# A two-layer convolution trunk on one core: stores of prepared weights and results moved to ScalarE's queue, layer 1's outputs moved behind its products

## The chip, the cores and the metric

One core of a Trainium2 chip runs the whole program in one launch. The metric is device time in microseconds (us), the median of three runs. The profile is one further execution of the same program.

## What is computed

x is 2048 rows by 1024 columns, c one row of 1024; all is float32. Two layers, then the output:

```python
cond = silu(c)
for l in (0, 1):
    shift, scale, gate = split(cond @ ada_w[l] + ada_b[l])      # 1024 each
    u = x * (1 + scale) + shift
    if l == 0:                                                  # "A"
        a, g, z = split(u @ W_in + b_in)                        # three of 1024 columns
        h = conv31(a * sigmoid(g)) + b_conv                     # causal, depthwise
        y = (silu(layer_norm(h)) * silu(z)) @ W_out + b_out
    else:                                                       # "B"
        b, c_, v, z = split(u @ W_in)                           # four of 1024 columns
        y = (b * conv3(c_ * v) * silu(z)) @ W_out
    x = layer_norm(sqrt(2) * x + gate * y) * g_post + b_post
```

## The kernel before

**Layout.** Columns lie on the 128 partitions, rows along the free axis. The 2048 rows are cut into two halves sc = 0, 1, each half into its even and its odd rows, which makes four quarters q = 2 sc + hf of T = 512 rows. The 1024 columns are 8 blocks of 128.

**A product.** Each matrix is done with one level of Strassen's scheme: a pair of column blocks (`Pair`, lines 236 to 348) needs 7 products instead of 8, of sums and differences of weight blocks (`make`, lines 255 to 293) and of sums and differences of u (`u_first`, `u_second`, lines 213 to 231: b11, b21, t1, t2, b22, t3, t4). Each operand is split into two float32r parts, hi by ScalarE and lo = operand - hi (`split`, line 184), so one product (`product`, line 350) is 4 blocks by 3 matmuls, 12 matmuls of 128x128 by 128x512. Layer A has 12 pairs of 7 products per half (8 pairs "a", 4 pairs "z"), layer B has 16 (8 "c", 8 "b"). The products write banks x, y, z of PSUM, of which there are four under the tag mm. After a product, `evacuate` (line 313) copies a bank with ScalarE or adds it with VectorE.

**Weights.** A pair's seven weight operands are built once, in half 0, from two raw loads (tag raw, 4 buffers), into buffers of the tag w (5 buffers), and stored to `kept` (line 291); half 1 loads them back. The sums of weight blocks run on GpSimd for layer A and on VectorE for layer B (`self.adds`, lines 245 and 982).

**The convolution of 31 taps** is cut into even and odd rows (`conv_a`, lines 457 to 543): 41 multiply-adds of VectorE for each of 8 blocks and each half (`mac`, line 467), with a few steps on ScalarE and GpSimd. They stand in a list, `todo`; `tick` (line 92) emits some of them after each product: 3 for layers A and B, 1 for an output step (`RATE`, line 34). When a block's accumulators are done, `statistics` (line 548) transposes them on TensorE and takes their sums on VectorE. When all 8 blocks of a quarter are done, `a_norm` (line 618) normalises it.

**Outputs.** `mixer_out` (lines 678 to 765) multiplies a quarter by W_out, 2 halves by 8 blocks by 12 matmuls, so 16 groups of the size of a product, adds the residual rows, normalises and stores; in layer 0 it also transposes the result (`columns`) into layer 1's u. W_out is first multiplied by the gate and split (`fold_gate`, line 425) into `w_dram`. `ada_sum` (line 397) makes a row of the modulation; both run as a background generator, one step for each product.

**Order of the program.** Start (lines 854 to 873): four rounds i, each with the loads of ada_w (`adak`), `modulation_a(i)` (line 373, 32 matmuls of one column), transposes of x, `u_parts`, and the first three products of pair 0 for the block before. Then the products of A for half 0 (A0), the input of half 1 (`u_half`, four times between the last products), A for half 1 (A1), outputs of quarters 0 and 1 of layer 0, B for half 0 (B0, with the gate of layer 1 folded in the background), then output of quarter 0 of layer 1, quarters 2 and 3 of layer 0, quarter 1 of layer 1, B for half 1 (B1), quarters 2 and 3 of layer 1.

**Queues.** Every transfer, loads and stores, is issued by SyncE (`load`, line 64, and `store`, line 73). Each engine and each queue works through its instructions in order. The order on all engines but TensorE is set by a scheduler from the order in the text, with `urgent` parts (line 76) first; TensorE keeps the order of the text.

## Time and profile before

| | us |
|---|---|
| median of 3 runs (1825.81 to 1827.89) | 1826.01 |
| the profiled execution | 1821.89 |
| its span, first to last instruction | 1820.1 |
| TensorE busy | 1602.8 (88%) |
| VectorE busy | 1161.4 (64%) |
| GpSimd busy | 1001.6 (55%) |
| ScalarE busy | 662.3 (36%) |

TensorE's mean granted clock is 0.941. The 16 transfer engines are busy 74.5% with the one queue that the kernel uses. A busy TensorE is no measure of how fast it works, since its matmuls take twice as long at the lower clock; so the stretches are read against the number of products in them.

### The profile page before, as it was taken

How to read it: one execution, taken by the hardware profiler on the slowest of the kernel's cores; microseconds unless marked ns; L12 is line 12 of the kernel's file. 1: busy time of each engine (PE TensorE's matmuls, PEld its weight loads, DVE VectorE, ACT ScalarE, POOL GpSimd, SP SyncE). 2: the span in 40 equal slices, each digit the busy share in tenths (PEclk: the TensorE clock that was granted, in tenths of full speed). 3: DMA queues.
4: the chain of work that ended last, by engine and by line, in shares of the span. 5: the costliest groups of instructions: out<-in, count | busy, mean ns of one | idle time of the engine just before them, and what ended most of it. 6: DMA issues, size and time to landing. Idle time of an engine off the chain costs nothing.

```text
span 1820.1 us, 21371 instructions
## 1 busy us (share of the span) xinstructions
PE 1602.8 (88%) x6956; PEld 1303.9 (72%) x6956; DVE 1161.4 (64%) x1737; ACT 662.3 (36%) x1134; POOL 1001.6 (55%) x868
## 2 busy tenths in 40 slices
PE   4989998789797977849878789998898999999995
PEld 4968787668676866737656568876677788888784
DVE  2329999978685899488988776457556321221264
ACT  2335455563342243464433233423643111111221
POOL 4268889476653254768877777727864211111243
PEclk9789999889898998979999899999999999999998
DMA  6558888779896896736777788899876666666865
GB/s 185 178 193 301 298 296 323 252 261 359 323 394 196 288 336 229 234 145 206 263 252 273 248 300 290 285 350 337 311 262 205 205 207 208 203 209 209 314 246 194
DMA packets 230719, 471.76 MB, mean 259 GB/s; under 512 B 20312, under 2 KB 94416, under 8 KB 230608
## 3 DMA queue, kind: packets, MB, share of 16 engines
q1 hardware_dynamic: 230608, 470.40, 74.5%
q8 instruction: 55, 0.90, 0.2%
q14 instruction: 56, 0.46, 0.1%
HBM read 299.81 MB, written 170.52 MB: 258 GB/s over the span
## 4 chain that ended last, share of the span: by engine, by line
PE 49%; DVE 18%; DMA 13%; POOL 10%; issue 6%; ACT 3%; SPq 1%; POOLq 0%; DVEq 0%; ACTq 0%
PE po L80 9%; PE pxc L80 7%; PE pxb L80 6%; PE pxa L80 6%; DVE pca L467 4%; PE pzc L80 4%; PE pzb L80 3%; PE pza L80 3%; DVE pcb L467 3%; PE pxz L80 2%; PE pm L80 2%; PE pya L80 2%; PE pyb L80 1%; PE pyc L80 1%; DMA wr<-w_dram 1%
## 5 line engine op out<-in xcount | busy, mean ns | idle before, releaser
L467 DVE SCALAR_TENSOR_TENSOR pcb<-h,w,pcb 128x512 f32<-128x512 f32 x224 | 166.7, 744 | 6.6 <-ACT pcb L475 6.4
L467 DVE SCALAR_TENSOR_TENSOR pca<-h,w,pca 128x512 f32<-128x512 f32 x192 | 142.9, 744 | 0.2
L467 DVE SCALAR_TENSOR_TENSOR pca<-xs,w,pca 128x512 f32<-128x512 f32 x128 | 95.6, 746 | 0.3
L728 DVE TENSOR_TENSOR r<-po,r 128x512 f32<-128x512 f32 x64 | 43.2, 679 | 80.0 <-issue 33.0
L793 POOL TENSOR_TENSOR hb1c<-c12c,c22c 128x512 f32<-128x512 f32 x16 | 22.1, 1384 | 130.9 <-DVE c22c L326 130.9
L467 DVE SCALAR_TENSOR_TENSOR pcd<-xs,w,pcd 128x512 f32<-128x512 f32 x112 | 83.5, 745 | 3.1 <-ACT pcd L509 3.1
L706 ACT ACTIVATE r<-r,nb,rs 128x512 f32<-128x512 f32 x64 | 47.7, 807 | 90.0 <-DVE nb L701 90.0
L412 POOL TENSOR_TENSOR ada<-ada,adaw 128x512 f32<-128x512 f32 x48 | 64.9, 1354 | 12.0 <-ACT adaw L406 10.2
L80 PE MATMUL pm<-cond,adak 128*128 128x1 f32 x256 | 49.0, 327 | 19.6 <-DMA adak<-in_ada_w_dram 19.6
L80 PEld LDWEIGHTS pm<-cond,adak 128*128 128x128 f32 x256 | 48.9, 298 | 20.3 <-DVE ua00t L220 10.1
L186 POOL TENSOR_TENSOR wa<-rawa,wa 128x512 fp32r<-128x512 f32 x32 | 42.1, 1322 | 28.0 <-ACT wa L185 28.0
L442 POOL TENSOR_TENSOR wf<-wf,grow 128x512 f32<-128x512 f32 x32 | 43.8, 1374 | 23.1 <-DMA wf<-in_b_w_out_dram 11.7
L481 POOL TENSOR_TENSOR lead<-lead,part 128x512 f32<-128x512 f32 x32 | 42.8, 1337 | 20.7 <-ACT part L480 20.7
L406 ACT ACTIVATE adaw<-adaw,cond 128x512 f32<-128x512 f32 x64 | 42.7, 715 | 31.6 <-DMA adaw<-in_ada_w_dram 25.9
L694 POOL TENSOR_TENSOR r<-r,gb 128x512 f32<-128x512 f32 x32 | 42.1, 1330 | 21.4 <-DVE pcb L467 11.0
L707 POOL TENSOR_TENSOR r<-r,g 128x512 f32<-128x512 f32 x32 | 49.8, 1566 | 3.9 <-ACT r L706 3.9
L721 ACT ACTIVATE ub<-ptx,sh,sc 128x128 f32<-128x128 f32 x128 | 46.7, 472 | 14.0 <-PE ptx L83 14.0
L186 POOL TENSOR_TENSOR wc<-rawc,wc 128x512 fp32r<-128x512 f32 x32 | 43.5, 1360 | 13.0 <-ACT wc L185 12.6
L186 POOL TENSOR_TENSOR wb<-rawb,wb 128x512 fp32r<-128x512 f32 x32 | 43.1, 1347 | 11.9 <-ACT wb L185 11.9
L647 ACT ACTIVATE v<-v,second_columns 128x512 f32<-128x512 f32 x32 | 25.8, 814 | 61.8 <-DVE v L646 51.5
L708 POOL TENSOR_TENSOR r<-r,b 128x512 f32<-128x512 f32 x32 | 47.7, 1499 | 0.6
L186 POOL TENSOR_TENSOR wf<-wf 128x512 fp32r<-128x512 f32 x32 | 43.9, 1377 | 6.2 <-ACT wf L185 6.2
(1385 smaller groups left out, 5570.5 us busy)
## 6 DMA issues: line engine op xcount, KB each, us to landing
wr<-w_dram SPq DMA_DIRECT2D x128, 512.0 KB, 5.1
kepta<-wa SPq DMA_DIRECT2D x56, 512.0 KB, 4.8
wa<-kepta SPq DMA_DIRECT2D x56, 512.0 KB, 6.5
keptc<-wc SPq DMA_DIRECT2D x56, 512.0 KB, 3.2
keptb<-wb SPq DMA_DIRECT2D x56, 512.0 KB, 4.5
wc<-keptc SPq DMA_DIRECT2D x56, 512.0 KB, 4.4
wb<-keptb SPq DMA_DIRECT2D x56, 512.0 KB, 4.3
adaw<-in_ada_w_dram SPq DMA_DIRECT2D x32, 512.0 KB, 7.2
```

Source lines behind the costliest of these rows:

```text
L80: return tc.keep_in_program_order(nc.tensor.matmul(*args, **kw))
L186: (eng or nc.gpsimd).tensor_tensor(lo, src, hi.bitcast(F32), op=ALU.subtract)
L406: nc.scalar.activation(raw[:, j], raw[:, j], AF.Identity, scale=cond[:, kk + j:kk + j + 1])
L412: nc.gpsimd.tensor_tensor(acc, acc, raw[:, j], op=ALU.add)
L442: nc.gpsimd.tensor_tensor(w[:, 1], w[:, 1], grow, op=ALU.mult)
L467: nc.vector.scalar_tensor_tensor(out=tiles[out], in0=src, scalar=w, in1=tiles[acc], op0=ALU.mult, op1=op)
L481: nc.gpsimd.tensor_tensor(lead, lead, part, op=ALU.add)
L706: nc.scalar.activation(r, r, AF.Identity, scale=rs, bias=nb)
L707: eng.tensor_tensor(r, r, g[h], op=ALU.mult)
L708: eng.tensor_tensor(r, r, b[h], op=ALU.add)
L721: nc.scalar.activation(fs[k][:, t * P:(t + 1) * P], pt[:, j * P:(j + 1) * P], AF.Identity, scale=sc1[:, k:k + 1], bias=sh1[:, k:k + 1])
L728: nc.vector.tensor_tensor(r, pss[t], r, op=ALU.add)
```

## The change

Seven things are changed together.

1. `store_late` and `flush`: the stores of kept weights, of `h_dram`, `z_dram`, `cc_dram`, `gb_dram` and `w_dram` (326 in all) are collected and issued by ScalarE, behind the next evacuation or activation in the text. The stores of accumulators and of output rows stay with SyncE. The zero windows of `h_dram` (16 stores) move in the text to the end of the start.
2. `modulation_a`: VectorE multiplies four of the eight blocks by cond and adds them; TensorE does the other four and the sum, 20 matmuls in place of 32. Each adak load holds one block of rows and both m.
3. The input of x is loaded in blocks of one column block (`u_block`). For half 1 its 16 blocks are spread over the last eleven products of A0 (`second_u`, `moves`); the last two pairs of every list are interleaved (`order_of`); four products, not three, run beside the start (`early`). The rows of the tables of columns and taps are loaded a round or more ahead, into the tag acc, not uf.
4. The subtraction for t2 moves from VectorE to GpSimd (`u_second`). In layer 1, `u_stages` makes all t1, then all t2, and so on, on VectorE and GpSimd in turn, and six products of B stand ahead of it in place of four.
5. In B0, two of the four weight sums of a pair move from VectorE to GpSimd. The second raw load of a pair is issued when its first sum is due.
6. The rate of the convolution is 3.2 steps a product in A, 3.4 in B; h has one buffer in place of two. `a_norm` of a half's first quarter runs within the last eleven products (`ending`), and the transposes of an output in layer 0 come 9 and 6 ticks behind its rows, not 6 and 4. The background of A1 takes two ticks for each step of `ada_sum`.
7. Layer 1's gate is folded during B1, and all four quarters of layer 1 are put out after B1.

```diff
+    def store_late(dst, src, then=None):
+        late.append((dst, src, then))
+    def flush(after=None):
+        with ExitStack() as order:
+            if after is not None:
+                order.enter_context(tc.issue_after(after.ins))
+            for dst, src, _ in late:
+                nc.scalar.dma_start(dst, src)
+        for *_, then in late:
+            if then is not None:
+                then()
+        late.clear()
...
-BUFS = dict(u=56, raw=4, s=1, w=5, ta=8, hin=2, xs=1, pt=1, acc=3, tv=2, uf=6)
+BUFS = dict(u=56, raw=4, s=1, w=5, ta=8, hin=1, xk=2, xs=1, pt=1, acc=3, tv=2, uf=6)
-RATE = dict(a=3, b=3, o=1)
+RATE = dict(a=3.2, b=3.4, o=1)
...
-                store(keep[n], wt.bitcast(F32))
+                store_late(keep[n], wt.bitcast(F32))
...
-                    nc.scalar.copy(t[key], bk[b])
+                    done = nc.scalar.copy(t[key], bk[b])
...
+                flush(done)
...
     def modulation_a(i):
         pm = bank("conv", f"pm{i}")
+        raws = []
+        for j in range(K):
+            raw = st("u", [P, 2, 2 * P], f"adak{i}_{j}")
+            load(raw, ada_w[0, j * P:(j + 1) * P, :2 * D].rearrange("p (m d) -> p m d", m=2)
+                 [:, :, 2 * i * P:(2 * i + 2) * P])
+            raws.append(raw)
+        acc = raws[0]
+        with urgent():
+            nc.vector.tensor_scalar(acc, acc, cond[:, :1], None, op0=ALU.mult)
+            for j in range(1, 4):
+                nc.vector.scalar_tensor_tensor(out=acc, in0=raws[j], scalar=cond[:, j:j + 1],
+                                               in1=acc, op0=ALU.mult, op1=ALU.add)
         for m in range(2):
             for b in range(2):
                 o = m * 2 + b
-                for j in range(K):
...
+                for j in range(4, K):
+                    matmul(pm[:, o:o + 1], raws[j][:, m, b * P:(b + 1) * P],
+                           cond[:, j:j + 1], start=(j == 4), stop=False)
+                matmul(pm[:, o:o + 1], acc[:, m, b * P:(b + 1) * P], ones[:, :1],
+                       start=False, stop=True)
...
-            U["t2"].append(u_tile(b11, name + "t2", nc.vector))
+            U["t2"].append(u_tile(b11, name + "t2"))
...
-                    tt(s, a12, s, op=ALU.subtract)
+                    tt2(s, a12, s, op=ALU.subtract)
...
-                    tt(a11, a11, a21, op=ALU.subtract)
+                    tt2(a11, a11, a21, op=ALU.subtract)
...
+        c, a, b = n - 3, n - 2, n - 1
+        return seq + [(c, 3), (a, 1), (c, 7), (b, 1), (c, 4)] + [
+            (a, 2), (b, 2), (a, 5), (a, 6), (a, 3), (b, 5), (b, 6), (b, 3),
+            (a, 7), (b, 7), (a, 4), (b, 4)]
...
+    moves = {(late_b, 2): 2, (late_a, 5): 2, (late_a, 6): 1, (late_a, 3): 1, (late_b, 5): 1,
+             (late_b, 6): 1, (late_b, 3): 2, (late_a, 7): 1, (late_b, 7): 1, (late_a, 4): 2,
+             (late_b, 4): 2}
...
+    for pair in pb[0]:
+        pair.adds = (nc.vector, nc.gpsimd)
+    rows = ending(pb[0], with_join(0, order_b), RATE["b"], 2)
+    need(3)
+    run_out(0, 2, wait(6, norms[3]))
+    begin_out(3, 0, rows)
+    run_out(0, 3, wait(10, join_first(1)))
     back = background_b()
+    for n, (p, r) in enumerate(with_join(1, order_b)):
+        if (p, r) == (n_b - 1, 5):
+            rows = out_rows(0, 1)
...
+        product(pb[1][p], r)
+        tick(0, *([back] if n > 8 else ()))
+    flush()
+    for q in range(NQ):
         begin_out(q, 1, rows)
+        if q:
+            b_gate(q, gs[1, q])
         run_out(1, q)
```

**SyncE's queue at the start**, round 0 to round 1 (adak is ada_w, xkua is x, rawa raw weights, kepta the store of a prepared weight). Before:

```order
L71 DMA rawa0_0_1_253<-in_a_w_in_dram 128x8x128
L74 DMA kepta0_0_250<-wa0_0_1_256 128x1024
L74 DMA kepta0_0_250<-wa0_0_2_260 128x1024
L74 DMA kepta0_0_250<-wa0_0_5_265 128x1024
L74 DMA kepta0_0_250<-wa0_0_6_687 128x1024
L71 DMA adak1_0_0_270<-in_ada_w_dram 128x2x256
```

Now:

```order
L71 DMA rawa0_0_1_239<-in_a_w_in_dram 128x8x128
L74 DMA h_dram0_89<-zero_104 128x15 x2
L74 DMA h_dram1_90<-zero_104 128x15 x2
L74 DMA h_dram2_91<-zero_104 128x15 x2
L74 DMA h_dram3_92<-zero_104 128x15 x2
L74 DMA h_dram4_93<-zero_104 128x15 x2
L74 DMA h_dram5_94<-zero_104 128x15 x2
L74 DMA h_dram6_95<-zero_104 128x15 x2
L74 DMA h_dram7_96<-zero_104 128x15 x2
L71 DMA adak1_0_247<-in_ada_w_dram 128x2x256
```

The four weight stores no longer stand ahead of round 1's ada_w; the 16 zero stores, which stood ahead of round 0's, stand there now.

**VectorE at the start**, round 0 to round 1 (ua00 is u of round 0, mod0 the modulation). Before:

```order
L220 TENSOR_TENSOR ua00t4_244<-ufua00_1_199,ufua00_0_192 128x512
L186 TENSOR_TENSOR ua00t2l_236<-ufua00_0_192,ua00t2h_235 128x512
L186 TENSOR_TENSOR ua00t4l_247<-ua00t4_244,ua00t4h_246 128x512
L391 TENSOR_TENSOR mod0_122<-pm1_269,ab0_123 128x2 x2
```

Now:

```order
L252 TENSOR_TENSOR ua00t4_224<-ufua00_1_177,ufua00_0_168 128x512
L219 TENSOR_TENSOR ua00t4l_227<-ua00t4_224,ua00t4h_226 128x512
L455 TENSOR_SCALAR adak1_0_247<-adak1_0_247,cond_85 128x512
L457 SCALAR_TENSOR_TENSOR adak1_0_247<-adak1_1_249,cond_85,adak1_0_247 128x512
L457 SCALAR_TENSOR_TENSOR adak1_0_247<-adak1_2_251,cond_85,adak1_0_247 128x512
L457 SCALAR_TENSOR_TENSOR adak1_0_247<-adak1_3_253,cond_85,adak1_0_247 128x512
L469 TENSOR_TENSOR mod0_106<-pm1_246,ab0_107 128x2 x2
```

The four new operations of a round stand behind the last operation on u of the round before, and TensorE's pm1 needs their result.

**ScalarE at the first products of A0** (kepta is now its own; c11, c12, c22 are evacuations). Before:

```order
L322 ACTIVATE c11a0_0_675<-pxa0_0_385,half_b_131 128x512
L185 CAST wa1_0_1_730<-rawa1_0_0_725 128x512
L185 CAST wa0_0_7_749<-rawa0_0_0_251 128x512
L320 COPY c22a0_0_684<-pza0_0_393 128x512
```

Now:

```order
L88 DMA kepta1_0_371<-wa1_0_1_374 128x1024
L385 COPY c22a0_0_685<-pza0_0_366 128x512
L387 ACTIVATE c11a1_0_690<-pxa1_0_370,half_b_115 128x512
L218 CAST wa0_0_3_712<-sa0_0_241 128x512
L218 CAST wa0_0_7_729<-rawa0_0_0_231 128x512
L387 ACTIVATE c12a0_0_708<-pxa0_0_358,half_b_115 128x512
L88 DMA kepta0_0_230<-wa0_0_6_693 128x1024
```

A weight's store stands behind an evacuation, in front of the next casts; SyncE's queue has 822 rows in place of 1140 and ScalarE's 1430 in place of 1104.

## Rows read from the trace of the kernel before

**Rows 1.** Busy time by stretch: us; PE, PEld, DVE, ACT, POOL; clock; DMA, GB/s

```profile
0.00:107.00 107.00, 76.31 (x360) 70.07 (x361) 35.10 (x50) 32.20 (x53) 37.19 (x37) 0.84 0.53 165
107.00:312.50 205.50, 203.76 (x907) 166.76 (x906) 174.60 (x275) 98.31 (x168) 174.05 (x141) 1.00 0.84 296
312.50:391.00 78.50, 54.59 (x229) 44.03 (x228) 76.39 (x109) 48.22 (x81) 46.95 (x37) 0.83 0.71 241
391.00:651.00 260.00, 233.55 (x1028) 191.88 (x1027) 195.70 (x335) 100.83 (x158) 128.59 (x108) 0.94 0.89 320
651.00:774.00 123.00, 102.56 (x444) 82.54 (x443) 96.03 (x155) 50.74 (x92) 71.77 (x63) 0.93 0.74 251
774.00:827.00 53.00, 28.20 (x99) 19.71 (x98) 42.06 (x45) 32.37 (x70) 36.40 (x28) 0.71 0.36 134
827.00:1187.60 360.60, 315.30 (x1325) 249.02 (x1324) 277.89 (x395) 139.78 (x240) 278.49 (x238) 0.95 0.77 270
1187.60:1820.10 632.50, 588.54 (x2577) 479.88 (x2575) 263.58 (x378) 159.88 (x277) 228.12 (x221) 0.97 0.73 246
137.00:1187.60 1050.60, 907.95 (x3890) 729.08 (x3889) 858.13 (x1303) 459.58 (x786) 713.34 (x593) 0.93 0.78 276
```

**Rows 2.** Chain that ended last, one product of B0: start, us, what

```profile
1080.26 2.72 PE pxc L80 x12
```

**Rows 3.** SyncE's queue, waits in total: us, times, longest

```profile
SPq L74 <- POOL wc L186: 85.5, 41, 7.1
SPq L74 <- POOL wb L186: 84.7, 41, 6.6
SPq L74 <- POOL wa L186: 75.0, 40, 8.9
```

**Rows 4.** Line 74, one store's issue: ns least/median/most, first and last start

```profile
L74 SPq DMA_DIRECT2D kepta<-wa x56: 319/320/1645, 25.0 to 318.4; - x56
```

**Rows 5.** Timeline of SyncE's queue, first 45 us: start, us, what

```profile
1.54 7.47 SPq L74 DMA_DIRECT2D h_dram<-zero  x16
9.05 4.02 SPq L71 DMA_DIRECT2D adak<-in_ada_w_dram  x8
25.02 11.91 SPq L74 DMA_DIRECT2D kepta<-wa  x4
36.98 4.45 SPq L71 DMA_DIRECT2D adak<-in_ada_w_dram  x8
```

**Rows 6.** Timeline of rounds 1 to 3 at the start: start, us, what

```profile
51.70 3.55 PE L80 MATMUL pm<-cond,adak 128*128 128x1 f32 x16
62.09 11.70 PE L80 MATMUL pm<-cond,adak 128*128 128x1 f32 x64
62.13 1.64 DVE L220 TENSOR_TENSOR ufua<-ufua,ufua 128x512 f32<-128x512 f32 x1
63.80 0.69 DVE L220 TENSOR_TENSOR ua01t<-ufua,ufua 128x512 f32<-128x512 f32 x1
65.49 1.34 DVE L186 TENSOR_TENSOR ua01t4l<-ua01t,ua01t4h 128x512 fp32r<-128x512 f32 x1 [0.34 <-ACT ua01t4h L185]
100.83 0.44 PE L83 MATMUL ptc<-ident,rt 124*128 124x124 f32 x1 [6.81 <-DMA rt<-in_a_conv_w_dram]
```

**Rows 7.** TensorE's waits over the whole run: us in total, times, longest

```profile
PE pmb L80 <- POOL ada L412: 22.2, 3, 9.3
PE pxc L80 <- ACT wc L185: 20.2, 3, 9.3
PE pm L80 <- DMA adak<-in_ada_w_dram: 19.6, 3, 9.7
```

**Rows 8.** Groups by shape, whole run: busy us, mean ns, idle before

```profile
L786 DVE SCALAR_TENSOR_TENSOR ccc<-hb1c,second_columns,ccc 128x512 f32<-128x512 f32 x32 | 30.0, 939 | 10.1 <-ACT ccc L784 9.2 <-POOL wf L442 0.8
L285 DVE TENSOR_TENSOR rawc<-rawc,rawc 128x512 f32<-128x512 f32 x8 | 10.3, 1286 | 0.1
L283 POOL TENSOR_TENSOR sa<-rawa,sa 128x512 f32<-128x512 f32 x8 | 11.4, 1427 | 0.2
```

More of the change, by code (lines that the diff above doesn't have):

```diff
@@ L129, in place_columns, with load_rows @@
             o += m
-    def load_columns(gi, g, ct=None):
-        n = sum(r[2] for r in g)
-        rt = st("uf", [P, P], f"rt{gi}")
+    rows_in = {}
+    def load_rows(gi, g):
+        rt = st("acc", [P, P], f"rt{gi}")
         o = 0
@@ L137, in load_columns @@
             o += m
+        return rt
+    def load_columns(gi, g, ct=None):
+        n = sum(r[2] for r in g)
+        rt = rows_in.pop(gi) if gi in rows_in else load_rows(gi, g)
         pt = bank("conv", f"ptc{gi}")
@@ L172, in hybrid_trunk, with zero_windows @@
     nc.gpsimd.memset(zero, 0.0)
-    for e in range(K):
-        for hf in range(2):
-            store(h_dram[e][:, hf, :HA], zero)
+    def zero_windows():
+        for e in range(K):
+            for hf in range(2):
+                store(h_dram[e][:, hf, :HA], zero)
     quarters = lambda ap: ap.rearrange("(s m two) d -> s two m d", s=2, two=2)
@@ L885, in background @@
         modulation_b(0, 1, res[1, 0, 1])
-        yield from ada_sum(1, 1, 0, res)
-        yield from ada_sum(1, 1, 1, res)
-        for n in range(10):
+        yield from slowly(ada_sum(1, 1, 0, res))
+        yield from slowly(ada_sum(1, 1, 1, res))
+        for n in range(5):
             yield
@@ L959, in need, with ending @@
             tick(4)
-    l = n_a - 1
-    for p, r in head + order_of(n_a):
-        if (p, r) == (l, 5):
-            rows = out_rows(0, 0)
-            begin_out(0, 0, rows)
-        product(pa[1][p], r)
-        queue_convs()
-        normed = p == l and r in (5, 6, 7, 3, 4) or (p, r) == (l - 1, 4)
-        tick(RATE["a"], back, *([norms[0]] if normed else ()))
-    for gen in (norms[0], back):
-        for _ in gen:
-            pass
+    def ending(pairs, order, rate, q, *beside):
+        a, b = len(pairs) - 2, len(pairs) - 1
+        gens = list(beside)
+        for p, r in order:
+            if (p, r) == (b, 5):
+                rows = out_rows(q, 0)
+            if (p, r) == (a, 6):
+                need(q)
+                gens.append(norms[q])
+            product(pairs[p], r)
+            queue_convs()
+            tick(rate, *gens)
+        for gen in gens:
+            for _ in gen:
+                pass
+        flush()
+        begin_out(q, 0, rows)
+        return rows
@@ L973, in hybrid_trunk @@
+    rows = ending(pa[1], order_a, RATE["a"], 0, back)
     need(1)
[L974 removed]
+    run_out(0, 0, wait(6, norms[1]))
     begin_out(1, 0, rows)
[L976 to L988 removed]
@@ L989, in hybrid_trunk @@
-    for _ in back:
-        pass
-    need(2)
-    begin_out(0, 1, out_rows(0, 1))
-    b_gate(0, gs[1, 0])
-    run_out(1, 0, wait(3, norms[2]))
-    need(3)
-    rows = out_rows(2, 0)
-    begin_out(2, 0, rows)
-    run_out(0, 2, wait(3, norms[3]))
-    begin_out(3, 0, rows)
-    b_gate(1, gs[1, 1])
-    run_out(0, 3, wait(7, join_first(1)))
-    begin_out(1, 1, out_rows(1, 1))
-    run_out(1, 1)
-    join(1)
-    pb = pairs_b(1, US[1, 1])
-    for p, r in start + order_of(n_b, 1):
-        product(pb[p], r)
-        tick(0)
@@ L1009, in hybrid_trunk, with with_join @@
-    rows = out_rows(2, 1)
-    for q in (2, 3):
+    run_out(0, 1, wait(10, join_first(0)))
+    start = [(0, 1), (0, 2), (1, 1), (1, 2), (2, 1), (2, 2), (0, 5), (0, 6), (0, 3), (0, 7),
+             (1, 5), (0, 4), (1, 6)]
+    pb = [pairs_b(sc, US[1, sc]) for sc in range(2)]
+    n_b = len(pb[0])
+    order_b = start + [at for at in order_of(n_b, 1) if at not in start]
+    for sc in range(2):
+        pb[sc][2].tags["y"] = "tp"
+    def with_join(sc, order):
+        for n, at in enumerate(order):
+            if n == 6:
+                join(sc)
+            yield at
```

245 lines of the change are left out of this document (146 added, 99 removed).

## The prediction

> **What bounds the kernel now.** I read the busy times by stretch first [rows 1], and set each stretch against the work in it. A product on a busy TensorE takes 2.72 us [rows 2], and so does one of the 16 groups of an output. The rest of a stretch is what TensorE did not spend on these: waiting, matmuls at the lower clock, transposes and small sums.
>
> | stretch | length | products and groups | rest |
> |---|---|---|---|
> | start | 107.0 | 3 | 98.8 |
> | A0 | 205.5 | 73 | 6.9 |
> | turn from A0 to A1 | 78.5 | 13 | 43.1 |
> | A1 | 260.0 | 79 | 45.1 |
> | outputs of quarters 0, 1, layer 0 | 123.0 | 32 | 36.0 |
> | first products of B0 | 53.0 | 6 | 36.7 |
> | B0 | 360.6 | 106 | 72.3 |
> | from there to the end | 632.5 | 208 | 66.7 |
>
> So 339 of the 405.6 us of rest lie in the first 1187.6 us, where the same work stands before and after the change, but for the folding of layer 1's gate. The reader is to see two other things there. TensorE waits for sums of GpSimd in A1 and for prepared weights in B0 [rows 7]; the weights come late because SyncE, in order, waits 245 us in front of the stores of other weights (85.5 + 84.7 + 75.0, [rows 3]), with raw loads queued behind. And VectorE works through the convolution all the while: from its start at 137 to the end of B0 it is busy 858.1 of 1050.6 us, 82% [rows 1]. It is the engine that can take TensorE's place as the bound.
>
> **Start (98.8 us of rest).** The first load of ada_w is issued at 9.05, behind 7.5 us of zero stores; the second at 36.98, behind 11.9 us in which SyncE waits for four prepared weights [rows 5]. Both waits go from there, though the zeros now hold the second load. Against that, VectorE's four new operations stand behind u of the round before. In round 1, pm ends at 55.25 and the last operation on u ends at 66.83 [rows 6]: 11.6 us later. The four operations add about 3 (0.69 each where nothing disturbs them, [rows 6]), then 16 of 20 matmuls remain, 32 of the 64 records that took 11.7 us [rows 6], so 5.9. A round is then 20 us or so, and between 55.25 and 73.79, the ends of pm in rounds 1 and 2, it is 18.5 now. The rounds gain nothing in themselves, whatever TensorE saves. What is gained is their earlier begin. I estimate the second pm's end at 40 for 55.25: its load is issued some 18 us earlier (SyncE at 1.5 + 4.0 + loads of x and weights, 6, + zeros, 7.5 = 19 for 36.98), and the chain of round 0 gives back a few. Two rounds of 20 put the fourth pm's end at 80, and the last u 11.6 later. The 6.8 us wait for the tap rows [rows 6], which would come there, is gone, since these are loaded early. So the first product behind the start moves from 107 to 92. There a new wait comes in: the sixth operand needs a buffer whose store ScalarE issues only behind the first evacuation, some 3.5 us. The start also holds one product more, 2.7. In sum 15 - 3.5 + 2.7 = **14 us gained**; bounds 0, if a round takes 25, and 25, if VectorE's chain hides.
>
> **A0.** 6.9 us of rest, nothing to gain. VectorE is busy 174.6 of 205.5 [rows 1], with its first 30 us spare; at 3.2 steps for 3 it stays just below TensorE. 0, bounds -5 and +10.
>
> **Turn (43.1).** Four clumps of 16 transposes, each waiting for ScalarE and for buffers, are spread as 16 small ones over eleven products, with buffers of their own, and one subtraction of a round leaves VectorE. TensorE has 2.72 us of work to cover each. Some 6 us of transposes stay, and about 10 of the chain of the last round: 16. **27 gained**, bounds 0 and 37.
>
> **A1 (45.1).** 22.2 us are waits for the modulation's sums on GpSimd [rows 7], and the granted clock of 0.94 costs 0.06 x 260 = 15.6 [rows 1]; a wait and the slow matmuls behind it are one thing. The sums now have twice the ticks, and their transfers no longer queue behind stores. I leave 17 for transposes and a VectorE that is nearly full. **28 gained**, bounds 0 and 40.
>
> **Outputs of quarters 0 and 1 (36.0).** The norm ends earlier and the transposes come later; the change of banks from the first to the second half of columns stays. **10 gained**, bounds -10 and 25.
>
> **First products of B0 (36.7).** The wait is for t1 and its followers, which now come four at a time, with half of their splits on GpSimd, and six products cover instead of four. But the last transposes stand just ahead of the sixth product, so the chain from there to t1 (evacuation, four subtractions of 0.69 to 1.64 [rows 6], cast and split) still shows: I leave 19. **18 gained**, bounds 0 and 30.
>
> **B0 (72.3).** The weights' waits (20.2 us for one line alone, [rows 7]) lose their cause. VectorE loses 32 of its sums at 1.29 us [rows 8], 41 us, and GpSimd takes them at 1.43, 46 us; it also loses the folding, and was busy 278.5 of 360.6 [rows 1]. What comes instead: 3.4 steps a product fill VectorE, and a buffer of weights is free only after ScalarE has issued its store, up to two products later; five buffers last 5 x 2.72 = 13.6 us. I leave 38. **34 gained**, bounds -20 and 60.
>
> **ScalarE.** 326 stores at 0.32 us [rows 4] are 104 us on an engine that works 662. They stand behind evacuations, where their data are ready, so I cost them at nothing; the cover is its idle time.
>
> **The rest of the run (66.7).** Layer 1's quarters 0 and 1 move behind B1; folding moves into B1, where ScalarE, GpSimd and VectorE are nearly idle. Six quarters and 112 products stay, and so do the two half-covered joins. **0**, bounds -15 and +15.
>
> **Sum.** 14 + 0 + 27 + 28 + 10 + 18 + 34 + 0 = 131 us off the profiled execution's 1821.9, so 1691. The median of the runs is 4.1 above that execution; I forecast **1695 us**. A check by VectorE: B0 would end at 1187.6 - 131 = 1056.6, the convolution start near 129, and it must be over some 35 us before the end of B0. VectorE has 858.1 - 41 and less about 17 for these last us, so 800 us of work in 893: 90% busy. That is possible in a stretch like A0, where it is full after its first 30 us, but not easy across an output stretch.
>
> **Rivals.**
> - *VectorE is the bound.* For it: 800 us at 85% need 941, so B0 ends at 129 + 941 + 35 = 1105, 82 us earlier than now; at the 82% of today it is 1140, 48 earlier. Against it: much of its present idle time is TensorE's waiting. 1744 (1778 at 82%).
> - *The start gains nothing.* VectorE's in-order chain makes a round 25 us. 1695 + 14 = 1709.
> - *GpSimd stands in VectorE's way.* The same subtraction of two operands in SBUF took 1.64 us while GpSimd was running and 0.69 when not [rows 6]. With more on GpSimd, B0's 32 convolution steps of this kind could go from 0.94 [rows 8] to 1.64, 22 us, and the 32 sums that stay from 1.29 to 1.64, 11: on a full VectorE 33 us, so 1728. The Trainium skill, page "SBUF — State Buffer", section "Who interferes with whom", has the rule: a VectorE instruction with two SBUF inputs contends with a GpSimd instruction that reads SBUF, by an exclusive lock, and whichever issues second waits. By that rule, which the two durations bear out, moving sums to GpSimd buys less than their VectorE time.
> - *ScalarE takes over SyncE's waits.* If a store comes to the head of ScalarE's queue before GpSimd has finished its operand, the evacuations behind it wait, then PSUM's banks, then TensorE. SyncE's 245 us [rows 3] are the price at full; it decides from 131/245 = 53%. At two thirds, 163 us, the time is 1695 + 163 = 1858, slower than before. Against it: a product uses its operand before the evacuation that the store follows, so the operand is done by then; this fails only for stores of folded weights and of results.
>
> **Chances.** Forecast 0.60, start 0.12, VectorE 0.12, GpSimd 0.10, ScalarE 0.06. Faster by more than 0.2% (3.7 us, about what a measurement of this kernel can tell) in all but the last: 0.93, same 0.01, slower 0.06. For the range, the terms' bounds together reach 106 us below the forecast and far above it; not all of them fall on one side, so I take about half of the way down, 1645, and upward to between the two prices of the VectorE rival, 1765. Outside are the slower rival, VectorE at its present 82%, and a better case than half of the bounds.
>
> **What would show it.** Right: SyncE's waits for wa, wb, wc gone, with ScalarE not waiting for GpSimd in their place; the first full product at 90 to 98; B0's end near 1057; TensorE's clock near 1.0 in A1; VectorE busy 90% from 129 on. Wrong: pm waiting for adak's sum over 5 us a round (start); evacuations late behind GpSimd's lo parts (ScalarE); VectorE without a gap while TensorE waits for `c12`, `c22` or `hb0` (VectorE as bound); VectorE's two-operand steps at 1.6 us throughout (GpSimd).

## The result and the profile after

The changed kernel takes **1758.39 us** (median of 4 runs, 1756.17 to 1759.53), against 1825.91 us for the kernel before in the same session: a ratio of 0.9633, with a 95% interval of 0.961 to 0.9657. It is faster, by 67.5 us. The forecast was 1695 us, so half of the forecast gain is missing. The time lies in the range of 1645 to 1765, but, as will be seen, not for the reason that set the range's upper end.

The profiled execution has a span of 1757.7 us. Here are its busy times by stretch, as in [rows 1]: start, A0, turn and A1, outputs of quarters 0 and 1, B0 with its first products, the remainder, and the stretch of the VectorE check. The columns are length; busy us (instructions) of PE, PEld, DVE, ACT, POOL; granted clock; share of the transfer engines; GB/s.

```profile
0.00:98.60 98.60, 62.27 (x277) 55.27 (x277) 41.65 (x59) 31.36 (x52) 39.32 (x39) 0.84 0.54 154
98.60:303.60 205.00, 197.64 (x869) 159.40 (x870) 175.58 (x273) 97.58 (x161) 165.42 (x134) 1.00 0.82 294
303.60:619.90 316.30, 290.42 (x1278) 234.60 (x1276) 281.66 (x438) 151.53 (x244) 186.28 (x152) 0.96 0.90 322
619.90:741.40 121.50, 102.67 (x436) 81.65 (x437) 95.00 (x151) 47.83 (x87) 72.52 (x65) 0.93 0.79 270
741.40:1118.10 376.70, 334.01 (x1433) 263.32 (x1431) 288.33 (x428) 164.59 (x289) 296.67 (x254) 0.97 0.65 237
1118.10:1757.70 639.60, 592.00 (x2572) 479.28 (x2572) 270.97 (x363) 173.16 (x303) 299.47 (x271) 0.98 0.78 266
129.00:1118.10 989.10, 895.61 (x3888) 715.53 (x3886) 832.45 (x1278) 448.90 (x760) 696.96 (x584) 0.97 0.78 279
```

I take from each length the products in it at 2.72 us, as the prediction did. The products in these stretches are now 4, 70, 94, 32, 112 and 208 (against before, one product moved from A0 to the start and two to the turn). Turn and A1, and B0 and its first products, are put together, since the order inside them changed.

| stretch | rest before | rest after | gained | forecast gain |
|---|---|---|---|---|
| start | 98.8 | 87.7 | 11.1 | 14 |
| A0 | 6.9 | 14.6 | -7.7 | 0 |
| turn and A1 | 88.2 | 60.6 | 27.6 | 55 |
| outputs of quarters 0, 1 | 36.0 | 34.5 | 1.5 | 10 |
| B0 with its first products | 109.0 | 72.1 | 36.9 | 52 |
| the remainder | 66.7 | 73.8 | -7.1 | 0 |

The gains add up to 62.3 us, the difference of the two spans but for rounding (1820.1 - 1757.7 = 62.4). No term came out above its forecast.

Of TensorE's long waits in [rows 7], pmb's is 1.6 us now, that of pxc for `wc` 2.5, and that of pm for the loads of ada_w 11.4. There is a new one, for VectorE's sum of the modulation (waits over the whole run: total, times, longest):

```profile
PE pm L98 <- DVE adak L457: 19.5, 3, 7.6
PE pm L98 <- DMA adak<-in_ada_w_dram: 11.4, 3, 5.7
PE pmb L98 <- POOL ada L490: 1.6, 1, 1.6
```

ScalarE has new waits too. These are its waits in B0, 741.4 to 1118.1. `L218` is the cast that writes the hi part into a weight buffer; it waits until the store of the buffer's last content has landed:

```profile
ACT wb L218 <- DMA keptc<-wc: 37.8, 21, 4.0
ACT wc L218 <- DMA keptc<-wc: 21.4, 15, 3.3
ACT wc L218 <- DMA keptb<-wb: 19.4, 10, 4.3
...
ACT wb L218 <- DMA keptb<-wb: 7.7, 12, 1.2
```

These four are 86.3 us. TensorE's waits for prepared weights in the same stretch are 15.1 us in all; the longest lines of them are

```profile
PE pxb L98 <- POOL wb L219: 3.2, 1, 3.2
PE pzb L98 <- POOL wb L219: 3.1, 6, 1.0
PE pzc L98 <- POOL wc L219: 3.1, 5, 0.6
PE pxc L98 <- ACT wc L218: 2.5, 1, 2.5
```

A piece of ScalarE's timeline there shows the pattern (start, us, what; ACTq is its queue of issues). Two stores are issued behind an evacuation at 962.14, and the cast at 965.21 has waited for one of them to land:

```profile
962.14 0.59 ACT L385 COPY c11b<-pxb 128x512 f32<-128x512 f32 x1 [0.65 <-PE pxb L98]
962.20 0.33 ACTq L88 DMA_DIRECT2D keptc<-wc  x1
962.56 0.44 ACTq L88 DMA_DIRECT2D keptb<-wb  x1
965.21 0.62 ACT L218 CAST wc<-rawc 128x512 fp32r<-128x512 f32 x1 [2.48 <-DMA keptc<-wc]
```

SyncE's waits for GpSimd's parts of the weights did not go either. In B0 of the change they are 209.2 us (112.5 for `wb`, 96.7 for `wc`), now in front of raw loads instead of stores.

So two theories stood at the beginning of the experiments. Theory 1: weight buffers come free late, since a store is issued only behind an evacuation, and this costs A0 its 8 us and B0 the missing 15. Theory 2: VectorE is the bound, as the first rival had it, and what weights do is of no account.

### The profile page after: what moved, and what is told of

It reads as the page before. It is cut to its first block, busy times and chain, and to the rows that moved or that the text cites. A ratio compares the mean times of both kernels' runs of the same rounds, so it can differ in the third digit from the quotient of the medians.

```text
span 1757.7 us, 21022 instructions
## 1 busy us (share of the span) xinstructions
PE 1579.0 (90%) x6860; PEld 1273.5 (72%) x6860; DVE 1153.2 (66%) x1709; ACT 666.1 (38%) x1134; POOL 1059.7 (60%) x912
## 4 chain that ended last, share of the span: by engine, by line
PE 49%; DVE 19%; DMA 15%; POOL 6%; issue 5%; ACT 4%; SPq 1%; ACTq 0%; POOLq 0%; DVEq 0%
PE po L98 12%; PE pxc L98 7%; PE pxb L98 7%; PE pxa L98 4%; DVE pca L545 4%; PE pzc L98 4%; PE pzb L98 4%; DVE pcb L545 3%; PE pza L98 2%; DMA kepta<-wa 2%; PE pya L98 2%; PE pxz L98 2%; PE pyb L98 2%; DMA keptc<-wc 1%; DMA keptb<-wb 1%
## 5 line engine op out<-in xcount | busy, mean ns | idle before, releaser
L490 POOL TENSOR_TENSOR ada<-ada,adaw 128x512 f32<-128x512 f32 x48 | 64.4, 1342 | 38.2 <-ACT adaw L484 36.1
L219 POOL TENSOR_TENSOR gb_0l<-vb,gb_0h 128x512 fp32r<-128x512 f32 x4 | 5.2, 1292 | 91.1 <-ACT gb_0h L218 91.1
L219 POOL TENSOR_TENSOR wa<-rawa,wa 128x512 fp32r<-128x512 f32 x32 | 43.0, 1348 | 24.9 <-ACT wa L218 24.9
L484 ACT ACTIVATE adaw<-adaw,cond 128x512 f32<-128x512 f32 x64 | 42.4, 713 | 22.6 <-DMA adaw<-in_ada_w_dram 21.4
L219 POOL TENSOR_TENSOR wc<-rawc,wc 128x512 fp32r<-128x512 f32 x32 | 47.2, 1474 | 5.1 <-ACT wc L218 4.2
L729 ACT ACTIVATE v<-v,second_columns 128x512 f32<-128x512 f32 x32 | 25.7, 812 | 62.1 <-DVE v L728 60.1
L789 DVE TENSOR_TENSOR r<-r,g 128x512 f32<-128x512 f32 x32 | 39.4, 1238 | 6.9 <-ACT r L788 6.8
```

Of the source, the lines that this page charges most:

```text
L219: (eng or nc.gpsimd).tensor_tensor(lo, src, hi.bitcast(F32), op=ALU.subtract)
L484: nc.scalar.activation(raw[:, j], raw[:, j], AF.Identity, scale=cond[:, kk + j:kk + j + 1])
L490: nc.gpsimd.tensor_tensor(acc, acc, raw[:, j], op=ALU.add)
L789: eng.tensor_tensor(r, r, g[h], op=ALU.mult)
```

## The experiments

All rests below are worked out from each kernel's trace by the same landmarks (first full product, first transpose of the turn, first group of an output, first product of B0, first group of the next output, end). A rest comes from one profiled execution, while the executions of one kernel differ by 3 to 10 us, so differences of a few us between two rests say nothing by themselves. The columns are, after the median and the ratio to the kernel before in the same session, the rests of the start, A0, turn with A1, outputs of quarters 0 and 1, B0 with its first products, and the remainder.

| kernel | us | ratio (95%) | start | A0 | turn, A1 | out | B0 | remainder |
|---|---|---|---|---|---|---|---|---|
| before | | 1 | 98.9 | 6.8 | 88.6 | 35.4 | 109.2 | 66.8 |
| change | 1758.39 | 0.9633 (0.961-0.9657) | 87.7 | 14.6 | 60.6 | 34.5 | 72.1 | 73.9 |
| e1 kept stores by SyncE | 1728.5 | 0.9451 (0.9431-0.9471) | 88.8 | 5.5 | 63.9 | 21.9 | 57.8 | 76.5 |
| e2 almost no kept stores | 1733.71 | 0.9479 (0.9457-0.9501) | 88.0 | 4.8 | 66.9 | 25.3 | 53.5 | 73.7 |
| e3 six weight buffers | 1770.55 | 0.9686 (0.9669-0.9703) | 90.5 | 6.2 | 91.0 | 23.0 | 63.0 | 79.3 |
| e4 fewer taps | 1757.59 | 0.9616 (0.9592-0.964) | 88.1 | 20.9 | 56.1 | 23.4 | 74.0 | 75.1 |
| e5 = e1, folding in B0 | 1823.03 | 0.9989 (0.9972-1.0006) | 88.8 | 5.5 | 62.1 | 21.9 | 159.0 | 69.4 |
| e6 = e1, sums on VectorE | 1728.66 | 0.9469 (0.9444-0.9494) | 88.0 | 4.9 | 61.1 | 21.9 | 63.3 | 71.9 |
| e7 = e1, modulation on TensorE | 1715.93 | 0.9397 (0.9375-0.9419) | 79.4 | 5.8 | 65.6 | 24.4 | 55.0 | 72.4 |
| e8 = e1, joins as before | 1739.67 | 0.952 (0.9496-0.9543) | 87.7 | 5.5 | 63.6 | 22.1 | 62.5 | 82.5 |
| e9 = change, folding in B0 | 1854.47 | 1.016 (1.0127-1.0194) | 87.7 | 13.5 | 56.4 | 30.4 | 176.6 | 69.0 |
| e10 = before, kept stores late | 1856.39 | 1.0165 (1.0135-1.0195) | 90.0 | 20.2 | 91.3 | 36.1 | 142.5 | 64.7 |
| e11 = e7, two delays | 1737.68 | 0.9522 (0.9491-0.9552) | 79.1 | 4.9 | 80.4 | 33.0 | 51.9 | 72.1 |
| e12 = e5 without GpSimd's folding | 1806.3 | 0.9899 (0.9864-0.9934) | 87.9 | 5.4 | 63.4 | 22.0 | 138.7 | 71.2 |

### The late stores: e1, e2, e3 and e4

e1 changes one line of the change, in `make`:

```
-                store_late(keep[n], wt.bitcast(F32))
+                store(keep[n], wt.bitcast(F32))
```

> The changed kernel with one line undone: the prepared weights are stored by SyncE again, as soon as they are there; all other late stores stay with ScalarE. If the stores' move is what shortened B0, SyncE's waits for wa, wb and wc come back (245 us in all before), B0's rest goes from 35.9 us back towards 72, and the time rises by 20 to 40 us, to 1780 to 1800. If B0 was shortened by the other parts (sums shared with GpSimd, folding moved out), the time stays within 5 us of 1758, or falls, since ScalarE no longer waits for buffers whose stores were issued late.

1728.5 us: about 30 us *faster* than the change, where the forecast's reading called for 20 to 40 slower. SyncE's waits did come back, and in B0 they are longer than before. SyncE's and TensorE's waits in B0 of e1 (724.0 to 1086.4):

```profile
SPq L74 <- POOL wc L219: 110.8, 42, 8.9
SPq L74 <- POOL wb L219: 91.8, 43, 15.1
```

```profile
PE ptx L101 <- POOL r L790: 7.7, 1, 7.7
PE pxc L98 <- POOL ub00t2l L219: 4.4, 1, 4.4
PE pxb L98 <- DVE c22b L392: 4.2, 4, 1.2
PE pzb L98 <- DVE c12c L392: 4.1, 1, 4.1
```

SyncE waits 202.6 us in front of stores there, and none of TensorE's longer waits is for a prepared weight; all of them together are 0.5 us, for 15.1 in the change. ScalarE's waits for kept stores to land, 86.3 us in the change's B0, have one line left of any size:

```profile
ACT wc L218 <- DMA keptc<-wc: 3.8, 2, 3.4
```

What ScalarE lost comes back: A0's rest falls from 14.6 to 5.5, B0's from 72.1 to 57.8. The outputs of quarters 0 and 1 also lose 12.6 us, in which no prepared weight is stored; e3 and e4, which relieve other things, show the same fall, so I put it down to no one cause.

e2 stores only the first pair's weights of each layer, and half 1 loads those in place of all others:

```
-            if self.key in kept:
+            if self.sc:
...
-                    load(wt.bitcast(F32), kept[self.key][n])
+                    load(wt.bitcast(F32), kept[self.key[0] in 'cb'][n])
...
-                store_late(keep[n], wt.bitcast(F32))
+                if keep is not None:
+                    store_late(keep[n], wt.bitcast(F32))
```

> Leaves out the storing of all prepared weights but those of the first pair of each layer; the second half loads these in the others' place. Its weight buffers are free when the product has read them. Theory 1 (buffers come free late, since a store is issued only behind an evacuation): ScalarE's waits for kept stores, some 140 us, go, A0's rest falls from 15.0 to about 7, B0's from 35.9 to about 24, the time by about 20 us to 1738. Theory 2 (VectorE is full, TensorE waits for it whatever the weights do): within 5 us of 1758.

A0 falls to 4.8 and B0 to 53.5, the time to 1733.71: theory 1, by size and place. It is no faster than e1 (the intervals of the two ratios overlap), so a store that is issued at once costs nothing that these runs can tell, whatever SyncE waits for it. (e2 takes the transfers away as well, so of the two e1 is the cleaner.)

e3 gives the buffers another dose:

```
-BUFS = dict(u=56, raw=4, s=1, w=5, ta=8, hin=1, xk=2, xs=1, pt=1, acc=3, tv=2, uf=6)
+BUFS = dict(u=56, raw=4, s=1, w=6, ta=8, hin=1, xk=1, xs=1, pt=1, acc=3, tv=2, uf=5)
```

> Six weight buffers for five, paid for by one buffer of x's blocks in the turn (two to one) and one of the float temporaries (six to five). Theory 1: A0's rest falls from 15.0 to about 9 and B0's from 35.9 to about 26; the turn loses up to 7 us by the missing block buffer; in all 5 to 12 us faster, 1746 to 1753. Theory 2: no gain in A0 and B0, and the turn's loss alone, 1758 to 1765.

The gain came where theory 1 has it (A0 6.2, B0 63.0), but the memory had to be taken from elsewhere, and turn with A1 lost 30 us, not 7: TensorE waited 22.6 us for blocks of x there with one buffer for them (6.5 in the change), and 24.9 us for the modulation's sums on GpSimd (1.6 in the change). ScalarE still issues all the stores here, so the gain in A0 and B0 speaks for the number of buffers and against ScalarE's time for issuing. In all it is slower than the change, 1770.55.

e4 takes work from VectorE instead:

```
         def tap_e(r):
+            if r > LEAD and r % 2 == 0:
+                return
...
         def tap_o(r):
+            if r % 2 == 0:
+                return
```

> Leaves out 13 of the 45 VectorE steps of each of the 16 convolutions (taps 4, 6, .. 14 of the even ones, 2, 4, .. 14 of the odd ones), 16 x 13 x 0.743 = 154.5 us of VectorE; everything else is issued at the same points. Theory 2 (VectorE is the bound from the first convolution to B0's end): that stretch shortens by 40 us or more, to a time below 1720. Theory 1 (weight buffers): VectorE only idles more, the time falls by less than 15 us, to 1743 to 1758.

VectorE's busy time from 129 us to B0's end falls from 832.45 of 989.10 us to 691.81 of 982.10, as the row of e4 shows, and the time stays at 1757.59. Theory 2 falls for the change as it is; whether VectorE is the next limit once the late stores are gone was not tried.

```profile
129.00:1111.10 982.10, 886.82 (x3889) 714.12 (x3888) 691.81 (x1070) 448.42 (x759) 695.56 (x584) 0.97 0.78 281
```

### What shortened B0: e5, e6, e9 and e12

e1 leaves a question: SyncE waits longer in front of stores than in the kernel before, yet B0's rest is half of the one before (57.8 for 109.2). If its waits are not what made weights late, something else was removed. e5 puts layer 1's gate beside B0 again, in e1:

```
-    rows = ending(pb[0], with_join(0, order_b), RATE["b"], 2)
+    rows = ending(pb[0], with_join(0, order_b), RATE["b"], 2, late_start(background_b()))
...
-    back = background_b()
+    back = iter(())
```

(`late_start` lets nine steps pass first.)

> e1 (prepared weights stored by SyncE at once) with one more part undone: the sums and the folding of layer 1's gate run beside B0 again, from its tenth product on, and nothing beside B1. Theory F (it was the folding in B0, with its raw buffers, its loads and its GpSimd work, that made the weights late, not SyncE's waits): the rest of B0 with its first products goes from e1's 57.7 us back to 85 or more, B1's from 24.7 to about 12, the time to 1735 to 1755. Theory S (the shared sums were the gain): B0 stays within 10 us of 57.7 and B1 still gets shorter, so the time falls to 1715 to 1728.

1823.03 us, 94.5 more than e1, and more than theory F asked for. B0's rest is 159.0. In B0 (722.4 to 1186.0) TensorE waits for weights, and SyncE, besides its old waits, waits for the stores of folded weights to land (these are late stores as well) before it may load into the raw buffers that they leave:

```profile
PE pzc L98 <- ACT wc L218: 30.6, 6, 12.9
PE pzb L98 <- ACT wb L218: 18.7, 6, 5.5
PE pxc L98 <- ACT wc L218: 8.0, 1, 8.0
```

```profile
SPq L74 <- POOL wc L219: 110.7, 48, 9.0
SPq L74 <- POOL wb L219: 92.6, 37, 6.6
SPq L71 <- DMA w_dram<-wf: 40.0, 12, 5.7
```

SyncE's waits in front of stores of prepared weights are the same as in e1, 203.3 us; they are not what differs.

The traces show a path, and it is there in the kernel before as well. The gate's sums and its folding take their buffers from the same four as the raw weights. In B0 SyncE waits in front of loads until a folded weight has left such a buffer: 20.4 us in the kernel before, 40.0 in e5 (above), none in e1. The raw load is then late, and the first cast of a pair waits for it. The kernel before, SyncE and ScalarE in its B0, then ScalarE in e5's B0:

```profile
SPq L71 <- DMA w_dram<-wf: 20.4, 11, 4.1
ACT wc L185 <- DMA rawc<-in_b_w_in_dram: 16.0, 4, 5.1
ACT wb L185 <- DMA rawb<-in_b_w_in_dram: 15.8, 4, 5.9
```

```profile
ACT wb L218 <- DMA rawb<-in_b_w_in_dram: 12.7, 4, 5.8
```

In e1 ScalarE has no such wait. TensorE's four longest waits for a weight in B0 of the kernel before, 4.4 to 9.3 us, each stand right behind such a cast, and the last thing that SyncE waited for before it issued these four loads was a folded weight's store (three times) or GpSimd's sum for the gate (once).

e12 splits the price of the folding: its loads, stores and buffers stay, GpSimd's part of it is left out.

```
-                    nc.gpsimd.tensor_tensor(acc, acc, raw[:, j], op=ALU.add)
+                    if (l, m) != (1, 2):
+                        nc.gpsimd.tensor_tensor(acc, acc, raw[:, j], op=ALU.add)
...
+            if l == 0:
+                nc.gpsimd.tensor_tensor(w[:, 1], w[:, 1], grow, op=ALU.mult)
+                split(w[:, 1], wr[:, 0], wr[:, 1])
+            else:
+                nc.scalar.copy(wr[:, 0], w[:, 1])
```

> e5 (folding of layer 1's gate beside B0, 1823 us) with GpSimd's part of that folding left out: the sums behind the first of each half, the multiplications by the gate and the lo parts, some 44 instructions of 1.33 us or 58 us of GpSimd in B0. Its loads, its stores and its use of the four raw buffers stay. If it is the buffers, and the loads and stores through them, that make B0's weights late, the time stays at 1790 or more. If it is GpSimd's time, it falls to 1750 or less, near e1's 1728.

1806.3 us: GpSimd's time is some 17 of the 94 us. The other part, near 78, comes with the transfers and the four raw buffers that the folding shares with the raw weights. These were not told apart further; the folded weights' stores, which are issued late here and were not in the kernel before, may have a part in it.

e6 undoes the sharing of the weight sums, in e1: `pair.adds = (nc.vector, nc.vector)`.

> e1 with all weight sums of B0 on VectorE again (32 of them back from GpSimd, some 41 us of VectorE by the rows of before). Theory S: B0's rest with its first products goes from 57.7 to 75 or more, the time to 1745 or more. Theory F, and VectorE not the bound: within 6 us of e1, 1722 to 1735.

1728.66, the same time as e1. B0 itself is 5.5 us longer and the remainder shorter. GpSimd's help with the sums bought nothing here.

e9 is the change with the edit of e5, to close the square.

> The change as it is (prepared weights stored late by ScalarE) with the sums and the folding of layer 1's gate beside B0 again, as in e5. It closes the square of two parts: the change 1758, e1 1728 (stores by SyncE at once), e5 1823 (the same with the folding in B0). If the late stores are the remedy for weights that queue behind SyncE's waits, they help where the folding's loads are in B0 too: this kernel stays below 1790 us, well under e5. If folding in B0 costs its 90 us by raw buffers and GpSimd's time, whoever stores the weights, it comes to 1830 or more.

1854.47. The folding's price is the same with either way of storing: the ratio goes from 0.9633 to 1.016 here and from 0.9451 to 0.9989 in e1 and e5.

### The late stores by themselves: e10

The kernel before with the prepared weights put into a list, which ScalarE issues behind the next evacuating copy:

```
-                store(keep[n], wt.bitcast(F32))
+                late.append((keep[n], wt.bitcast(F32)))
...
+                flush(done)
```

> The kernel before with that part alone: its prepared weights are stored by ScalarE, each behind the next evacuation. If SyncE's waits of 245 us made weights late there, B0's rest falls from 72.5 us by 20 or more and the start's 11.9 us of SyncE's waits go too: 1785 to 1805. If late freed buffers cost as much as they do in the change (9 us in A0, some 20 in B0), the time is the same or slower, 1820 to 1855.

1856.39 us, slower than before by 1.35 to 1.95%. The start gains 8.9 us, for SyncE no longer waits there, but A0's rest goes from 6.8 to 20.2 and B0's from 109.2 to 142.5. TensorE's waits in B0 that the forecast had put down to SyncE did not go; that for `wc` is longer than in [rows 7], that for `wb` was 7.2 us before:

```profile
PE pxc L90 <- ACT wc L195: 24.4, 3, 9.0
PE pxb L90 <- ACT wb L195: 13.5, 2, 8.8
```

The casts here wait for late stores to land, and they still wait for raw loads, though SyncE no longer stands in front of prepared weights' stores:

```profile
ACT wb L195 <- DMA rawb<-in_b_w_in_dram: 13.1, 3, 8.5
```

SyncE is not free in e10, for it waits 63.2 us in B0 in front of the stores of folded weights. So e10 alone does not show that its waits are harmless; e1 does.

So there are three pairs, with and without late stores: 0.9633 for 0.9451, 1.016 for 0.9989, 1.0165 for 1. Each time they cost between 1.6 and 1.9%, 30 us or so. The totals agree better than their parts: A0 and B0 together, where the weights are stored, lose 23.4, 25.6 and 46.7 us. In the first two pairs the outputs of quarters 0 and 1 lose 12.6 and 8.5 us more and the turn with A1 gains some; in the third the start gains 8.9.

### The start and the joins: e7 and e8

e7 gives the first modulation back to TensorE, in e1, with the change's loads; VectorE's four steps go:

```
...
-                for j in range(4, K):
-                    matmul(pm[:, o:o + 1], raws[j][:, m, b * P:(b + 1) * P],
-                           cond[:, j:j + 1], start=(j == 4), stop=False)
-                matmul(pm[:, o:o + 1], acc[:, m, b * P:(b + 1) * P], ones[:, :1],
-                       start=False, stop=True)
+                for j in range(K):
+                    matmul(pm[:, o:o + 1], raws[j][:, m, b * P:(b + 1) * P],
+                           cond[:, j:j + 1], start=(j == 0), stop=(j == K - 1))
```

> e1 with the first modulation on TensorE alone again (32 matmuls a round, VectorE's four steps gone; loads and their order as in the change). If VectorE's chain sets the round (the start rival), the first full product stays at 97 to 101 us or comes earlier, and the time is 1722 to 1730. If TensorE's matmuls set it, each of four rounds is longer by some 5 us and the time is about 1745.

1715.93 us, 12.6 below e1, and the best of all kernels here. The first full product comes at 90.3 us, for 99.7 in e1. TensorE's last modulation in the change, and in e7:

```profile
72.37 0.95 PE L98 MATMUL pm<-cond,adak 128*128 128x1 f32 x8
80.93 0.58 PE L98 MATMUL pm<-ones,adak 128*128 128x1 f32 x2 [7.62 <-DVE adak L457]
81.38 1.85 PE L98 MATMUL pm<-cond,adak 128*128 128x1 f32 x8
...
87.35 0.56 PE L98 MATMUL pm<-ones,adak 128*128 128x1 f32 x2
```

```profile
69.97 9.02 PE L98 MATMUL pm<-cond,adak 128*128 128x1 f32 x64
```

40 matmul records take 15.5 us there, 64 take 9.0 here. It waits 7.62 us for VectorE's sum in the first of four columns, and then its small matmuls run at half the pace (1.85 us for eight records that took 0.95 ahead of the wait).

e8 makes the operands at the joins pair after pair again, in e1:

```
...
-        u_stages(US[1, sc], *halves, f"ub{sc}")
+        for i in range(KH):
+            f0, f1 = (fu[2 * sc + h][2 * i:2 * i + 2] for h in range(2))
+            u_second(US[1, sc], f0, f1, f"ub{sc}{i}")
```

> e1 with the operands at the two joins made pair after pair again, in the order before (t1, b22, t2, t3, t4 of one pair, then of the next), with six products ahead as in the change. If the staged order is worth what the forecast gave it, B0's rest with its first products goes from 57.7 to about 75 and B1's from 24.7 to 35, the time to 1750 or more. If the six products ahead of it did all of it, within 6 us of e1.

1739.67: the staged order is worth 11 us, 4.7 of it in B0 and 6.0 in the remainder, where B1's join stands. Both readings missed: it is neither nothing nor twenty.

### Two delays: e11

```
-        for n in range(5):
+        for n in range(10):
...
-                defer(6 if q % 2 else 9, lambda: columns(t))
+                defer(4 if q % 2 else 6, lambda: columns(t))
```

> e7 (stores by SyncE at once, modulation on TensorE alone) with two more edits that touch different stretches: in A1 the last two modulations come five products later (ten steps for five, as before), and in the outputs of layer 0 the transposes of a finished block come after 6 and 4 steps, as before, for 9 and 6. If TensorE waits in A1 only because these sums are not ready, pmb's part of A1's rest (14.6 us) falls below 5. If the later transposes were a gain, the rest of the outputs of quarters 0 and 1 with B0's first products (43.5 us) grows by 5 to 15; if they were none, it falls by as much. In all 1700 to 1725.

Slower than e7, 1737.68. TensorE's waits for GpSimd's sums in A1 (12.0 us in e7) are gone, but now one modulation stands behind the norm of quarter 0 in A1 (351.8 to 621.4), and TensorE waits for it in one piece:

```profile
PE pmb L98 <- DVE v L719: 30.1, 1, 30.1
```

So the change's earlier place was the better one: turn with A1 is 80.4 us for 65.6. The transposes' place is hardly to be told: outputs and B0 together are 84.9 us for 79.4, and part of that may be the norm's delay.

## Why the prediction was right in sign and too high in size

**ScalarE's stores, "I cost them at nothing"**: this step failed, and of the shortfalls that a run isolates it is the largest. The issues do take the forecast 0.33 us each and lie beside other work. What they cost is the age of a buffer: issued late, the store lands late, the cast into that buffer waits, and the weight is late. Price some 30 us in three pairs, of which 23.4 us lie in the change's A0 and B0; the 12.6 us in the outputs are not explained by it. The prediction had named the mechanism ("a buffer of weights is free only after ScalarE has issued its store"), and put it only into B0's term, where B0 still was to gain 34; for A0 and its five buffers it had nothing. The Trainium skill, page "DMA: Bandwidth & Descriptors", section "Issuing engines are not separate DMA queues", says that issuing from several engines saves only the time to initiate a transfer. The runs agree in that the stores of wa, wb and wc landed on the whole no sooner from ScalarE (medians 4.1, 5.2 and 3.3 us from issue to landing in the change) than from SyncE (4.8, 4.5 and 3.2 before; 3.7, 3.1 and 3.1 in e1). And the time that ScalarE's issues took over was worth nothing here: SyncE waited 202.6 us in e1's B0, and that cost nothing that shows.

**B0, "the weights' waits lose their cause"**: the size was right once the late stores are away (e1 leaves 57.8 where the forecast had 57), the cause was wrong. SyncE's waits in front of stores of prepared weights were not what made the weights late: e1 has more of them without harm, and in e10 the raw loads are late without them. What bears the weight is the folding of layer 1's gate, which left B0: 94 us by e1 and e5, in the changed program. In the kernel before it can have cost no more than part of its 109.2, as there its stores were not late; that it alone makes the 51 us between before and e1 was not tried, since layer 1's first output stands right behind B0 there. That it had a part in the kernel before is shown by the raw loads, which come late there and in e5 and not in e1. The shared sums and the staged join are about 5.5 and 4.7 us of the 51 (e6, e8); the later second raw load and the rate of 3.4 were not tried alone. The forecast listed the folding only as GpSimd's and VectorE's relief. The term for VectorE's sums (41 us moved to GpSimd) is worth nothing in the whole time by e6, where B0's rest is 5.5 us longer and the remainder 4.6 us shorter.

**Start, 14**: it came to 11.1, by errors that in part cancel. The second modulation ended at 43.75 for 40, and the later rounds took 22 us, not 20 (VectorE's four operations 3.8 us for 3, the matmuls behind them 7.0 for 5.9). That makes 7.9 us too late. Some of it comes back, for the wait of 3.5 us for the sixth operand is not there: TensorE waits for no weight longer than 0.7 us around the first full products. The sentence "the rounds gain nothing in themselves, whatever TensorE saves" was too kind: VectorE's chain made them longer. Without it the rest is 79.4, a gain of 19.4. The second rival (VectorE's chain makes a round 25 us) named the right mechanism and gave it too high a price; the forecast, with a round of 20, was nearer to the 22 us.

**Turn and A1, 55**: 27.6, and no experiment got more than 32.5 (e4). The clumps of transposes did spread, but with two buffers for blocks of x TensorE still waits 6.5 us for x's loads, and A1 keeps waits on evacuations (3.5, 2.1 and 1.3 us). The wait for the modulation's sums did go, from 22.2 to 1.6 us, and the granted clock in A1 is 0.98 for 0.94. Which step of these two terms was mis-sized is open: all of TensorE's waits there that the profile shows are 26 us of the 60.6.

**Outputs of quarters 0 and 1, 10**: 1.5 in the change, but 10 to 13.5 in e1, e2, e3 and e4. What holds the gain back in the change is open.

**Remainder, 0**: it cost 7.1; the outputs in it became 6.1 us shorter, B1 longer. Of B1 with its first six products, 12.0 us of rest became 25.3, and 23.2 where the folding is not beside it (e5); so the folding is not the reason. In the kernel before, an output of layer 1 stood between the last transposed columns and B1's join. That output went to the end, and the join lost its cover. TensorE's longest waits in B1 are now for the join's operands (4.0 us for `ub11t2l`, 2.5 for `ub11t1l`), where the one that the profile lists before was for an evacuation (7.5 us). That this is the cause was argued from the order and these waits, not tried alone.

**Rivals.** VectorE as the bound is out for the change (e4). So it is luck that the time lies in the range: 1765, its upper end, stood between the two prices of this rival. GpSimd in VectorE's way was priced at 33 us; the convolution's two steps of layer B took 1.02 and 0.95 us for 0.94 [rows 8] and 0.91, the sums that stayed 0.88 to 1.06, shorter than [rows 8], and e6 moves the time by nothing. ScalarE taking over SyncE's waits had the right engine and the wrong wait: it hardly waits for GpSimd's operand, but for stores to land.

```profile
L868 DVE SCALAR_TENSOR_TENSOR ccc<-hb1c,second_columns,ccc 128x512 f32<-128x512 f32 x32 | 32.5, 1015 | 13.9 <-ACT ccc L866 13.7
```

Of the signs listed: SyncE's waits for weights are still there, in front of raw loads; TensorE's clock in A1 is 0.98 (near 1.0); the first full product at 98.6 (90 to 98 forecast), B0's end at 1118.1 (1057), VectorE busy 84% from 129 on (90%), and pm waiting 19.5 us for adak's sum in three rounds, the sign "over 5 us a round" that was to speak against the start.

A version that beats both kernels is e7, the change without its late stores of prepared weights and without VectorE's share in the modulation: 1715.93 us, 6.0% below the kernel before.

## What to carry to other kernels

An engine that waits in front of a store harms nobody unless somebody waits behind it: before a queue's waiting time is priced, look for the consumer that was late by it. Moving a store to a later place in another queue lengthens the life of its buffer, and with few buffers that is a wait on the engine that fills the next one. When several parts go in together, undo them one at a time; here two of them cost 42 us (1758.39 for 1715.93) that the others had to earn.

## What the hardware showed beyond this

At the join, GpSimd is held off by VectorE's steps with two operands in SBUF, and not only the other way round. Around 786 us in the change (VectorE's timeline, the first and the last of six such steps in a row, then GpSimd's; start, us, what):

```profile
785.13 0.68 DVE L344 TENSOR_TENSOR sb<-rawb 128x512 f32<-128x512 f32 x1
...
788.14 0.68 DVE L219 TENSOR_TENSOR ub01b22l<-ub,ub01b22h 128x512 fp32r<-128x512 f32 x1
```

```profile
785.79 4.16 POOL L219 TENSOR_TENSOR ub02t2l<-ub,ub02t2h 128x512 fp32r<-128x512 f32 x1 [4.14 <-ACT ub02t2h L218]
789.91 1.26 POOL L219 TENSOR_TENSOR ub00b22l<-ub,ub00b22h 128x512 fp32r<-128x512 f32 x1
```

VectorE runs on at 0.68 us a step, and the lo part on GpSimd takes 4.16 us where the next takes 1.26; it ends 1.13 us behind VectorE's last step. With both engines at work from 768.40 on, nine of VectorE's subtractions took 11.24 us, 1.25 each. In e1 TensorE pays for it: the lo part of `ub00t2` took 5.21 us from 770.2 on, and TensorE's wait of 4.4 us for it is the second in its list above. So what is split over both engines in such a stretch is hardly done in parallel, which may be why the staged join gave 11 us and not more. The Trainium skill, page "SBUF — State Buffer", section "Who interferes with whom", has it that the port that the two engines share is an exclusive lock, and that the order of issue decides who blocks. The trace agrees that one of them blocks; here GpSimd's instruction stood through five of VectorE's in a row, which is more than the section says.
